# A list scheduler that ranks by due time instead of program order, with durations as traced

## The chip, the cores and the metric

One core of a Trainium2 chip runs the whole kernel. The core has TensorE (PE, matmuls; PEld is its weight load), VectorE (DVE), ScalarE (ACT), GpSimd (POOL) and SyncE (SP), whose queue issues all of this kernel's DMAs. The metric is the time of one execution in device microseconds, as the median of the runs.

## The reference

One layer of an encoder over 1024 tokens of width 1024, in float32:

```python
for l in range(DEPTH):   # DEPTH = 1
    mod = (silu(c) @ ada_w[l] + ada_b[l]).reshape(B, 3, 3, D_MODEL)
    h = modulate(x, norm_g[l, 0], mod[:, 0, 0], mod[:, 0, 1])        # RMS norm, scale, shift
    x = x + 0.5 * mod[:, 0, 2] * swiglu(h, ffn1_w1[l], ffn1_w3[l], ffn1_w2[l])
    h = modulate(x, norm_g[l, 1], mod[:, 1, 0], mod[:, 1, 1])
    y = hybrid_mixer(h, ...)
    x = x + mod[:, 1, 2] * y
    h = modulate(x, norm_g[l, 2], mod[:, 2, 0], mod[:, 2, 1])
    x = x + 0.5 * mod[:, 2, 2] * swiglu(h, ffn2_w1[l], ffn2_w3[l], ffn2_w2[l])
```

The feed-forward width is 2816. The mixer projects h to queries, keys and values of two kinds of attention with 8 heads of 64 each: one with a forget gate and a causal mask ("fox"), one in which each query attends to the 256 keys with the highest index score (the top-k part, "dsa"). Their outputs go through a projection each, are weighted by sigmoid gates of h, added and projected again.

## The kernel before, in words

Every float32 product is made of three fp32r matmuls: an operand is split into a high part (`wh`, `h`, `yh`, `pth`; ACT copies it to fp32r) and a low part (`wl`, `yl`, `ptl`; DVE or POOL subtracts), and `mm3` issues high x high, high x low, low x high. A feed-forward product is made by Strassen's scheme with 7 instead of 8 block products, so DVE also adds and subtracts blocks of weights (`wr`, `a`, `s`), of operands (`t1` to `t4`) and of results (`z`, `u`).

The layer function describes the work in program order in five parts, each ended by a `flush`: the modulation and the first feed-forward, with the first projections of the mixer; index scores and the first two groups of fox heads; the other projections, half of the gates and the top-k search (`topk`, 32 rounds of counting on DVE and 33 on ACT); attention (`pt` transposes of probabilities, `pth` and `ptl` their split, `py` the value products), with the other half of the gates between (`gt`, whose matmuls write `py` tiles too) and the masks; the branches' projections (`wbr`, `d_y`), the mixer's output and the second feed-forward.

The program calls nothing directly. `Plan.take` (line 182) records each instruction as a `Task` with its predecessors, and gives it a rank: its place in program order plus `behind`, an amount by which some side work (modulation 150, gates and top-k 100, masks 600) is set back. `Plan.flush` (line 264) then places the tasks of its part one by one. For each engine it goes through up to 60 waiting tasks, ordered by rank, and picks the one that can start earliest; a later one in that order is taken only if it can start over 0.05 us earlier. Of the engines' picks the earliest is placed. The start is the latest of: the inputs' end, the engine's, the buffers' and, for DVE and POOL, the other's use of the shared port. A task that takes a new tile has to wait while its rank is over `window` (200, from the second part on 600) above the lowest rank not yet placed. `Plan.length` (line 246) gives the duration of an instruction, and 0.12 us are added before another engine may use the result. A DMA takes 1.3 us and its bytes at 345 KB per us, one after another, and 0.7 us. The order found is the order in which each engine gets its instructions; the chip waits on semaphores, not on the planned times. Nothing else depends on the plan but which buffer of a pool a tile gets.

All instructions are issued from one line, 358, so groups of the profile are told apart by their tiles.

Of the kernel before, what the change touches and what calls it, by code (L numbers as in the profile page):

```python
# [18 lines left out]
PSUM = bass.MemoryType.PSUM  # L19
# [36 lines left out]
class View:  # L56
# [53 lines left out]
    def real(self):  # L110
        t = self.tile.real()
        for name, a, kw in self.ops:
            t = t[a[0]] if name == "__getitem__" else getattr(t, name)(*a, **kw)
        return t
# [45 lines left out]
    return v.real() if isinstance(v, View) else v  # L160


class Plan:


# [16 lines left out]
    def take(self, engine, op, a, kw):  # L182
        if not self.on:
            return getattr(getattr(self.tc.nc, engine), op)(*map(real, a), **{n: real(v) for n, v in kw.items()})
        t = Task(len(self.tasks), engine, op, a, kw)
        t.rank = t.i + self.behind
        self.tasks.append(t)
        writes = [v for v in (a[0], kw.get("accum_out")) if isinstance(v, View)]
        reads = [v for v in list(a[1:]) + [w for n, w in kw.items() if n != "accum_out"] if isinstance(v, View)]
        before = set()  # L190
        for views, write in ((reads, False), (writes, True)):
            for v in views:
                r = v.region()
                for r2, j, w2 in v.tile.log:
                    if (write or w2) and j != t.i and all(p < q2 and p2 < q for (p, q), (p2, q2) in zip(r, r2)):
                        before.add(j)
        for views, write in ((reads, False), (writes, True)):
            for v in views:
                if write and not v.ops:
                    v.tile.log = []  # L200
                v.tile.log.append((v.region(), t.i, write))
        t.ready = max([getattr(v.tile, "written", 0.0) for v in reads] + [0.0])
        tiles = {id(v.tile): v.tile for v in reads + writes + self.wanted}
        self.wanted = []
        for x in tiles.values():
            if x.t is None and x.first is None:
                t.new.append(x)
                x.first = t.i
            elif x.t is None:
                before.add(x.first)  # L210
            x.uses += 1
        t.tiles = list(tiles.values())
        t.written = [v.tile for v in writes]
        for j in before:
            self.tasks[j].after.append(t)
        t.left = len(before)
        out = writes[0] if writes else a[0]
        shape = list(out.shape)
        t.n = int(np.prod(shape[1:]))
        if op == "tensor_reduce":  # L220
            t.n = int(np.prod(a[1].shape[1:]))
        t.bytes = 4 * int(np.prod(shape))
        t.port = engine in ("vector", "gpsimd") and "accum_out" not in kw and not any(
            v.tile.pool.space == PSUM for v in reads + writes)
        if engine == "tensor":
            m = a[2] if op == "matmul" else a[1]
            t.exact = m.tile.dt in (F32R, BF16) or any(o[0] == "bitcast" and F32R in o[1] for o in m.ops)
# [16 lines left out]
        return self.done.setdefault(x.key, [(0.0, i) for i in range(x.kw.get("bufs", 1))])  # L244

    def length(self, t, e):
        if e == "tensor":
            if t.exact:
                return max(0.08, t.n / 2250.0)
            if t.op == "transpose":  # L250
                return t.n / 860.0
            return max(0.24, t.n / 500.0)
        more = "accum_out" in t.kw
        if e == "scalar":
            return 0.1 + t.n / 1200.0 + (0.3 if more else 0.12 if any(isinstance(t.kw.get(x), View) for x in ("bias", "scale")) else 0.0)
        if e == "vector":
            if t.op == "tensor_tensor_scan":
                return 0.1 + t.n / 450.0
            return max(0.2, 0.08 + t.n / 960.0 + (0.18 if more else 0.06 if t.op == "scalar_tensor_tensor" else 0.0))
        if e == "gpsimd":  # L260
            return 0.1 + t.n / (900.0 if t.op == "tensor_scalar" else 440.0)
        return 0.35

    def flush(self, keep=()):

# [3 lines left out]
        tasks, free = self.tasks, self.free  # L269
        start = max(free.values())  # L270
        waiting = {e: [] for e in self.ENGINES}

        def release(t):
            insort(waiting[t.engine], t, key=lambda u: u.rank)

        for t in tasks:
            if not t.left:
# [7 lines left out]
        def slot(t):  # L285

            when, need = 0.0, {}
            for x in t.new:
                if x.kw.get("tag"):
                    need.setdefault(x.key, []).append(x)  # L290
            if need and t.rank > low + self.window:
                return None
            for s, xs in need.items():
                if xs[0].kw["bufs"] == 1 and news[s][0] != t.i:
                    return None
                got = sorted(self.slots(xs[0]))
                if len(got) < len(xs) + (0 if news[s][0] == t.i else min(self.spare, xs[0].kw["bufs"] // 4)):
                    return None
                when = max(when, got[len(xs) - 1][0])
            return when  # L300

        todo = sorted(tasks, key=lambda t: t.rank)
        while len(order) < len(tasks):
            best = None
            while todo[0].placed:
                todo.pop(0)
            low = todo[0].rank
            for e in self.ENGINES:
                w = waiting[e][:60]
                pick, ahead = None, 0.0  # L310
                for t in w:
                    room = slot(t) if t.new else 0.0
                    if room is None:
                        continue
                    s = max(t.ready, room, free[e])
                    if t.port:
                        s = max(s, self.port["gpsimd" if e == "vector" else "vector"])
                    if pick is None or s < pick[0] - 0.05:
                        pick = (s, t, e)
                if pick and (best is None or pick[0] < best[0]):  # L320
                    best = pick
            assert best, "no task can be placed: " + str([(t.engine, t.op, [x.kw for x in t.new]) for w in waiting.values() for t in w][:8])
            s, t, e = best
            d = self.length(t, e)
            end = s + d + 0.12
            if t.port:
                self.port[e] = s + d
            free[e] = s + d
            if e == "sync":
                self.wire = max(self.wire, s + 1.3) + t.bytes / 345e3  # L330
                end = self.wire + 0.7
                free[e] = max(free[e], self.wire - 5.0)
            t.placed = True
            order.append((s, len(order), t, e, d))
            waiting[e].remove(t)
            for x in t.new:
                if x.kw.get("tag"):
                    news[x.key].remove(t.i)
                    x.slot = min(self.slots(x))
                    self.slots(x).remove(x.slot)  # L340
                    x.slot = x.slot[1]
            for x in t.written:
                x.written = max(getattr(x, "written", 0.0), end)
            for x in t.tiles:
                x.uses -= 1
                x.end = max(getattr(x, "end", 0.0), end)
                if not x.uses and x.slot is not None:
                    self.slots(x).append((x.end, x.slot))
                    self.kept.pop(id(x), None)
            for u in t.after:  # L350
                u.left -= 1
                u.ready = max(u.ready, s + d if u.engine == e and e != "sync" else end)
                if not u.left:
                    release(u)
        self.trace = sorted(order, key=lambda o: o[:2])
# [151 lines left out]
def t512(k, dt=F32, name="t", home="c"):  # L507

    p, tag, n = k.homes[home]
    return p.tile([128, H], dt, tag=tag, name=name, bufs=n)  # L510
# [1057 lines left out]
class Down:  # L1568
# [34 lines left out]
    def sum(self, n, q):  # L1603
        a, nc = {m: t[q] for m, t in self.a.items()}, self.k.nc
        if n == "s3":
            self.any.tensor_sub(a["a11"], a["a11"], a["a21"])
        elif n == "s2":
            t = self.a["s2"][q] = t512(self.k, name="s2")
            self.any.tensor_sub(t, a["a22"], a["a11"])
        elif n == "s1":  # L1610
            self.any.tensor_add(a["a21"], a["a21"], a["a22"])
        elif n == "s4":
            self.any.tensor_sub(a["a12"], a["a12"], a["s2"])
# [665 lines left out]
```

## Time and profile before

| | |
|---|---|
| runs | 2271.02, 2266.53, 2259.95 us |
| median of the runs | 2266.53 us |
| span of the profiled execution | 2259.4 us |
| mean granted clock of TensorE | 0.989 |
| TensorE busy, matmuls | 2178.7 us, 10508 |
| weight loads busy | 1799.5 us |
| DVE busy, instructions | 1802.3 us, 3391 |
| ACT busy, instructions | 1101.8 us, 1996 |
| POOL busy, instructions | 268.6 us, 255 |
| HBM read, written | 237.53 MB, 76.28 MB |

The profile is of one more execution; its span runs from the first to the last instruction, and no time of its own is listed beside it. It is 7.1 us below the median of the runs and 0.6 us below the lowest. A row of a stretch gives its bounds in us from the span's start, its length, and for each engine the busy us and the instructions that started in it. Busy time of TensorE includes modelled ends of pipelined matmuls: its mean for one matmul of 512 columns is 396 ns, while 2618 of them start in 600 us.

### The profile page before, as it was taken

The numbers are of one execution on the slowest core, as the hardware profiler recorded it, in microseconds if no ns is written. First come the engines' busy times: TensorE is split into PE (matmuls) and PEld (weight loads), VectorE is DVE, ScalarE is ACT, GpSimd is POOL, SyncE is SP. The second block draws the span as 40 slices with busy tenths as digits, with TensorE's granted clock in tenths as the row PEclk, the third lists the DMA queues.
The fourth block names the chain that finished last, engine by engine and source line by source line (L and its number), as shares of the span: only waits on it lengthen the run. The fifth ranks groups of instructions, "written<-read, shape, count | busy, mean of one in ns | idle before, by whom it ended". The sixth has DMA issues, their size and how long they took to land.

```text
span 2259.4 us, 31187 instructions
## 1 busy us (share of the span) xinstructions
PE 2178.7 (96%) x10508; PEld 1799.5 (80%) x10508; DVE 1802.3 (80%) x3391; ACT 1101.8 (49%) x1996; POOL 268.6 (12%) x255
## 2 busy tenths in 40 slices
PE   7999999999999999998999999899999999999999
PEld 5777888787887989996778887687888888888887
DVE  7998987889775488888788877668898877769765
ACT  4432232344464476787687787423443333324443
POOL 0000000000010223323555433000000000000000
PEclk9999999999999999999999999999999999999999
DMA  9234554497421313334332210767223442258520
GB/s 336 81 114 161 168 173 131 146 367 238 126 74 61 121 61 122 113 122 136 107 110 89 76 35 20 278 239 256 87 80 131 135 133 96 93 179 319 168 75 38
DMA packets 187421, 315.89 MB, mean 140 GB/s; under 512 B 27366, under 2 KB 51942, under 8 KB 187260
## 3 DMA queue, kind: packets, MB, share of 16 engines
q1 hardware_dynamic: 187260, 313.89, 41.1%
q8 instruction: 83, 1.36, 0.2%
q14 instruction: 78, 0.64, 0.1%
HBM read 237.53 MB, written 76.28 MB: 139 GB/s over the span
## 4 chain that ended last, share of the span: by engine, by line
PE 45%; DVE 3%; ACT 2%; DMA 2%; issue 1%; SPq 0%; ACTq 0%; DVEq 0%; POOL 0%
PE b L358 34%; PE py L358 6%; PE pt L358 3%; PE p L358 2%; DVE macc L358 1%; DMA wr<-in_w_g 1%; DMA mraw<-in_ada_w 0%; ACT pth L358 0%; ACT pr L358 0%; DVE ptl L358 0%; ACT kst L358 0%; DVE qs L358 0%; DMA wr<-in_wbr 0%; ACT yt L358 0%; DVE kst L358 0%
## 5 line engine op out<-in xcount | busy, mean ns | idle before, releaser
L358 PE MATMUL b<-h,wh 128*128 128x512 f32 x2720 | 855.8, 396 | 10.0 <-ACT wh L358 5.0
L358 PEld LDWEIGHTS b<-h,wh 128*128 128x128 f32 x2720 | 511.9, 189 | 136.1 <-ACT wh L358 9.1
L358 PE MATMUL b<-h,wl 128*128 128x512 f32 x1360 | 533.7, 395 | 2.4 <-DVE wl L358 2.4
L358 ACT ACTIVATE wh<-wr 128x512 fp32r<-128x512 f32 (+2 forms) x368 | 245.5, 676 | 469.3 <-PE b L358 343.8
L358 PEld LDWEIGHTS b<-h,wl 128*128 128x128 f32 x1360 | 256.2, 188 | 64.2 <-DVE wl L358 4.2
L358 DVE TENSOR_TENSOR z<-b,z 128x512 f32<-128x512 f32 x308 | 207.3, 684 | 73.0 <-PE b L358 71.9
L358 PE MATMUL b<-wl,wh 128*128 128x512 f32 x616 | 241.8, 393 | 5.5 <-DVE wl L358 5.5
L358 PE MATMUL b<-wh 128*128 128x512 f32 x616 | 239.4, 391 | 2.5 <-ACT wh L358 1.7
L358 PE MATMUL b<-wh,wl 128*128 128x512 f32 x616 | 241.2, 392 | 0.0
L358 DVE TENSOR_TENSOR wl<-wr,wh 128x512 fp32r<-128x512 f32 x312 | 206.7, 683 | 32.9 <-ACT wh L358 32.8
L358 PE MATMUL pj<-wh,h 128*128 128x384 f32 (+1 forms) x768 | 179.5, 319 | 0.1
L358 ACT ACTIVATE wh<-a 128x512 fp32r<-128x512 f32 x132 | 83.3, 631 | 194.0 <-PE b L358 168.3
L358 POOL TENSOR_TENSOR wl<-wr,wh 128x1024 fp32r<-128x1024 f32 (+2 forms) x56 | 120.1, 2150 | 283.8 <-ACT wh L358 276.9
L358 DVE TENSOR_TENSOR wl<-a,wh 128x512 fp32r<-128x512 f32 x132 | 91.4, 693 | 76.8 <-ACT wh L358 76.8
L358 PEld LDWEIGHTS b<-wl,wh 128*128 128x128 f32 x616 | 116.6, 189 | 31.9 <-DVE wl L358 7.6
L358 PEld LDWEIGHTS b<-wh 128*128 128x128 f32 x616 | 116.1, 188 | 27.8 <-ACT wh L358 2.3
L358 PEld LDWEIGHTS b<-wh,wl 128*128 128x128 f32 x616 | 116.4, 189 | 24.6 <-DVE wl L358 0.4
L358 PEld LDWEIGHTS pj<-wh,h 128*128 128x128 f32 x768 | 132.4, 188 | 1.1 <-ACT wh L358 0.2
L358 DVE TENSOR_TENSOR z<-z 128x512 f32<-128x512 f32 x176 | 119.4, 690 | 10.7 <-DVE z L358 0.5
L358 PE MATMUL pj<-wl,h 128*128 128x384 f32 (+1 forms) x384 | 122.6, 319 | 0.5 <-POOL wl L358 0.5
L358 POOL TENSOR_SCALAR pr<-pr,mn 128x128 f32<-128x128 f32 (+7 forms) x128 | 101.2, 804 | 153.7 <-DVE mn L358 136.8
L358 DVE TENSOR_TENSOR wl<-g,wh 128x512 fp32r<-128x512 f32 x154 | 106.7, 695 | 0.0
(283 smaller groups left out, 3677.3 us busy)
## 6 DMA issues: line engine op xcount, KB each, us to landing
d_g<-z SPq DMA_DIRECT2D x154, 256.0 KB
g<-d_g SPq DMA_DIRECT2D x154, 256.0 KB
mraw<-in_ada_w SPq DMA_DIRECT2D x144, 256.0 KB
wr<-in_w13a SPq DMA_DIRECT2D x112, 256.0 KB
wr<-in_w13b SPq DMA_DIRECT2D x88, 256.0 KB
wr<-in_w_g SPq DMA_DIRECT2D x32, 512.0 KB
a<-in_w2a SPq DMA_DIRECT2D x44, 256.0 KB
a<-in_w2b SPq DMA_DIRECT2D x44, 256.0 KB
```

What stands on the lines that cost most here:

```text
L358: getattr(getattr(self.tc.nc, e), t.op)(*map(real, t.a), **{n: real(v) for n, v in t.kw.items()})
```

## The change

`flush` orders waiting tasks by a due time, `due`, in place of the rank. `deadlines` works it out before each part is placed. It goes through the tasks by rank and lays the matmuls and transposes end to end: one is due when the sum of the durations ahead of it says. Any other task is due 20 us (`SLACK`) after the matmuls ahead of it in rank. Then it goes backward: a task is due no later than the due time of each task that uses its result, less its own duration, less the time that a result takes to another engine, and for a DMA less 2.0 us and its bytes. A task that uses a tile whose buffer a later tile will take over (`soft`) is due ahead of the task that takes it. The rule of the 0.05 us, the 60 tasks, the window and the ranks themselves stay.

`length` returns two numbers, duration and time to another engine: for 512 columns a matmul takes 0.230 (before 0.228), a transpose of 128 columns 0.109 (0.149), a DVE operation on two tensors 0.603 (0.613), an ACT copy 0.537 (0.527). A result takes 0.23 us from TensorE, 0.16 from ACT, 0.145 from DVE, 0.105 from POOL (0.12 before, whatever the engine). ACT with a running sum takes 0.1 us more in place of 0.3. 0.03 us is added for each engine over one that a task waits for. A use on the same engine after a running sum waits 0.1 us. The shared port of DVE and POOL is now taken by a POOL task that reads more than 8 columns from SBUF, and by a DVE task that reads two such inputs from SBUF, or one in `tensor_scalar`, `tensor_copy` and `reciprocal`; before it was by every task of the two engines that has no PSUM tile and no running sum.

```diff
@@ -158,6 +158,9 @@
 
 def real(v):
     return v.real() if isinstance(v, View) else v
+SLACK = 20.0
 
 
 class Plan:
@@ -213,6 +216,7 @@
         t.written = [v.tile for v in writes]
         for j in before:
             self.tasks[j].after.append(t)
+        t.waits = len({self.tasks[j].engine for j in before} - {engine})
         t.left = len(before)
         out = writes[0] if writes else a[0]
         shape = list(out.shape)
@@ -220,8 +224,17 @@
         if op == "tensor_reduce":
             t.n = int(np.prod(a[1].shape[1:]))
         t.bytes = 4 * int(np.prod(shape))
-        t.port = engine in ("vector", "gpsimd") and "accum_out" not in kw and not any(
-            v.tile.pool.space == PSUM for v in reads + writes)
+        wide = [v for v in reads if int(np.prod(v.shape[1:])) > 8]
+        sb = [v for v in wide if v.tile.pool.space != PSUM]
+        if engine == "gpsimd":
+            t.port = bool(sb)
+        elif engine == "vector":
+            if op in ("tensor_scalar", "tensor_copy", "reciprocal"):
+                t.port = len(sb) == 1 and "accum_out" not in kw and writes[0].tile.pool.space != PSUM
+            else:
+                t.port = len(sb) >= 2
+        else:
+            t.port = False
         if engine == "tensor":
             m = a[2] if op == "matmul" else a[1]
             t.exact = m.tile.dt in (F32R, BF16) or any(o[0] == "bitcast" and F32R in o[1] for o in m.ops)
@@ -244,22 +257,84 @@
         return self.done.setdefault(x.key, [(0.0, i) for i in range(x.kw.get("bufs", 1))])
 
     def length(self, t, e):
+        n = t.n
+        if e == "sync":
+            return 0.06, 0.0
         if e == "tensor":
             if t.exact:
-                return max(0.08, t.n / 2250.0)
-            if t.op == "transpose":
-                return t.n / 860.0
-            return max(0.24, t.n / 500.0)
+                d = max(0.04, 0.009 + n / 2317.0)
+            elif t.op == "transpose":
+                d = n / 1174.0
+            else:
+                d = max(0.224, 0.009 + n / 595.0)
+            return d, 0.23
         more = "accum_out" in t.kw
         if e == "scalar":
-            return 0.1 + t.n / 1200.0 + (0.3 if more else 0.12 if any(isinstance(t.kw.get(x), View) for x in ("bias", "scale")) else 0.0)
-        if e == "vector":
-            if t.op == "tensor_tensor_scan":
-                return 0.1 + t.n / 450.0
-            return max(0.2, 0.08 + t.n / 960.0 + (0.18 if more else 0.06 if t.op == "scalar_tensor_tensor" else 0.0))
+            ap = sum(isinstance(t.kw.get(x), View) for x in ("bias", "scale"))
+            return 0.11 + n / 1200.0 + (0.1 if more else 0.0) + (0.06 if ap else 0.0), 0.16
         if e == "gpsimd":
-            return 0.1 + t.n / (900.0 if t.op == "tensor_scalar" else 440.0)
-        return 0.35
+            if t.op in ("tensor_scalar", "memset"):
+                return 0.08 + n / 960.0, 0.105
+            return 0.06 + n / 440.0, 0.105
+        if t.op == "tensor_tensor_scan":
+            d = 0.15 + n / 480.0
+        elif t.op == "tensor_tensor_reduce":
+            d = 0.17 + n / 960.0
+        elif t.op == "scalar_tensor_tensor" or more:
+            d = 0.13 + n / 960.0
+        elif t.op == "tensor_scalar" and t.port:
+            d = 0.075 + n / 1920.0
+        else:
+            d = 0.07 + n / 960.0
+        return max(0.2, d), 0.145
+    def deadlines(self):
+        tasks = self.tasks
+        at = 0.0
+        ordered = sorted(tasks, key=lambda t: t.rank)
+        for t in ordered:
+            t.len, t.lat = self.length(t, t.engine)
+            if t.waits > 1 and t.engine not in ("tensor", "sync"):
+                t.len += 0.03 * (t.waits - 1)
+            t.due = at + SLACK
+            if t.engine == "tensor":
+                t.due = at
+                at += t.len
+        users, frees, soft, born, ends, count = {}, {}, {}, {}, {}, {}
+        for t in ordered:
+            for x in t.tiles:
+                users.setdefault(id(x), []).append(t)
+        for t in ordered:
+            for x in t.new:
+                born[id(x)] = x
+        for n, t in enumerate(ordered):
+            t.pos = n
+        for i, ts in users.items():
+            ends.setdefault(ts[-1].pos, []).append(i)
+        for t in ordered:
+            for x in t.new:
+                if not x.kw.get("tag"):
+                    continue
+                q = frees.setdefault(x.key, [])
+                n = count.get(x.key, 0)
+                if n < x.kw["bufs"]:
+                    count[x.key] = n + 1
+                elif q:
+                    for u in users[q.pop(0)]:
+                        if u.pos < t.pos:
+                            soft.setdefault(u.pos, []).append(t)
+            for i in ends.get(t.pos, ()):
+                if i in born and id(born[i]) not in self.kept and born[i].kw.get("tag"):
+                    frees.setdefault(born[i].key, []).append(i)
+        for t in reversed(ordered):
+            d = t.due
+            for u in t.after:
+                d = min(d, u.due - t.len - (t.lat if u.engine != t.engine else 0.0) - (2.0 + t.bytes / 345e3 if t.engine == "sync" else 0.0))
+            for u in soft.get(t.pos, ()):
+                d = min(d, u.due - t.len - t.lat)
+            t.due = d
 
     def flush(self, keep=()):
 
@@ -269,9 +344,10 @@
         tasks, free = self.tasks, self.free
         start = max(free.values())
         waiting = {e: [] for e in self.ENGINES}
+        self.deadlines()
 
         def release(t):
-            insort(waiting[t.engine], t, key=lambda u: u.rank)
+            insort(waiting[t.engine], t, key=lambda u: u.due)
 
         for t in tasks:
             if not t.left:
@@ -321,8 +397,8 @@
                     best = pick
             assert best, "no task can be placed: " + str([(t.engine, t.op, [x.kw for x in t.new]) for w in waiting.values() for t in w][:8])
             s, t, e = best
-            d = self.length(t, e)
-            end = s + d + 0.12
+            d = t.len
+            end = s + d + t.lat
             if t.port:
                 self.port[e] = s + d
             free[e] = s + d
@@ -349,7 +425,7 @@
                     self.kept.pop(id(x), None)
             for u in t.after:
                 u.left -= 1
-                u.ready = max(u.ready, s + d if u.engine == e and e != "sync" else end)
+                u.ready = max(u.ready, s + d + (0.1 if "accum_out" in t.kw else 0.0) if u.engine == e and e != "sync" else end)
                 if not u.left:
                     release(u)
         self.trace = sorted(order, key=lambda o: o[:2])
```

## The prediction, made before the changed kernel ran

> **What bounds the kernel now.** I read the page's first part, then a table of stretches, then the groups by shape in the attention stretch, then the chain, the waits and the timeline at the places where TensorE stops.
>
> ```profile
> span 2259.4 us, 31187 instructions
> PE 2178.7 (96%) x10508; PEld 1799.5 (80%) x10508; DVE 1802.3 (80%) x3391; ACT 1101.8 (49%) x1996; POOL 268.6 (12%) x255
> ```
>
> TensorE is the bound, with 4% idle by this line. But a busy TensorE is not a dense one: ends of matmuls are modelled, and they overlap. So I count matmuls per stretch. Columns: length, then busy us (x instructions) of PE, PEld, DVE, ACT and POOL, granted clock, DMA share, GB/s.
>
> ```profile
> 0.00:28.00 28.00, 14.87 (x50) 6.34 (x51) 15.96 (x38) 10.43 (x17) 0.69 (x6) 1.00 0.94 338
> 28.00:100.00 72.00, 71.99 (x326) 59.61 (x325) 69.69 (x123) 36.25 (x63) 0.00 (x0) 0.98 0.56 192
> 100.00:250.00 150.00, 141.15 (x582) 110.23 (x581) 138.23 (x242) 48.73 (x82) 0.50 (x2) 0.97 0.40 134
> 550.00:850.00 300.00, 283.70 (x1405) 249.06 (x1404) 209.35 (x345) 159.15 (x271) 38.54 (x31) 0.99 0.29 95
> 1045.00:1075.00 30.00, 20.62 (x86) 16.33 (x85) 19.73 (x64) 20.42 (x37) 13.68 (x13) 0.81 0.42 139
> 1075.00:1370.00 295.00, 285.35 (x1799) 232.74 (x1798) 240.11 (x540) 221.65 (x472) 144.09 (x157) 1.00 0.26 80
> 1370.00:1421.00 51.00, 41.91 (x271) 34.77 (x268) 36.73 (x88) 35.48 (x80) 14.82 (x20) 0.97 0.09 23
> 1421.00:1428.00 7.00, 0.02 (x1) 0.02 (x1) 2.64 (x4) 3.14 (x6) 0.00 (x0) 0.56 0.91 292
> 1428.00:1560.00 132.00, 129.60 (x553) 104.31 (x553) 103.69 (x164) 46.75 (x77) 0.00 (x0) 0.98 0.82 284
> 1560.00:2160.00 600.00, 600.00 (x2618) 488.23 (x2617) 474.95 (x776) 225.13 (x371) 0.00 (x0) 1.00 0.42 143
> ```
>
> The stretch 1560:2160, the second feed-forward, is dense: 600 / 2618 = 0.229 us for a matmul of 512 columns. There no order of work can gain anything. At that pace 100:250 has room for 654 matmuls and holds 582: 72 x 0.229 = 16.5 us are lost, with VectorE busy 138 of 150 us, so VectorE is what TensorE waits for there. 1428:1560 has room for 576 and holds 553: 5 us lost. 550:850, where forms are mixed, has at least 300 - 283.7 = 16 us idle. 1045:1075 has 9 us idle, and the rest at 0.81 of the clock.
>
> In attention the count needs shapes. The groups of 1100 to 1400, kept apart by shape (count | busy us, mean ns | idle before):
>
> ```profile
> L358 PE MATMUL pt<-ident,pr 128*128 128x128 f32 x512 | 80.9, 276 | 4.9 <-DVE kst L358 2.1 <-DVE qs L358 1.5 <-DVE ptl L358 1.2
> L358 PE MATMUL py<-h,wh 128*128 128x512 f32 x202 | 71.0, 407 | 0.0
> L358 PE MATMUL py<-pth,vst 128*128 128x256 f32 x171 | 53.9, 322 | 2.1 <-ACT pth L358 1.8
> L358 PE MATMUL py<-ptl,vst 128*64 128x256 f32 x171 | 46.1, 292 | 1.4 <-DVE ptl L358 1.2
> L358 PE MATMUL py<-h,wl 128*128 128x512 f32 x101 | 41.6, 412 | 0.0
> L358 PE MATMUL py<-pzh,vst 128*128 128x256 f32 x112 | 34.1, 304 | 0.8 <-ACT pzh L358 0.5
> L358 PE MATMUL p<-kst,qs 128*128 128x512 f32 x84 | 28.1, 418 | 0.0
> L358 PE MATMUL py<-pzl,vst 128*64 128x256 f32 x112 | 23.0, 287 | 0.4 <-DVE pzl L358 0.4
> L358 PE MATMUL p<-kst,qs 128*128 128x384 f32 x84 | 21.7, 354 | 0.0
> L358 PE MATMUL p<-kst,qs 128*128 128x448 f32 x56 | 17.3, 396 | 0.0
> L358 PE MATMUL p<-kst,qs 128*128 128x320 f32 x56 | 13.2, 334 | 0.1
> L358 PE MATMUL pt<-ident,nat 128*128 128x128 f32 x68 | 11.6, 274 | 0.2
> ```
>
> A row of the chain of work that ended last prices a transpose (eight in 0.87 us, 0.109 each):
>
> ```profile
> 1249.90 0.87 PE pt L358 x8
> ```
>
> By columns at 0.229 per 512: 202 + 101 + 84 = 387 of 512, 89 us; 171 + 171 + 112 + 112 = 566 of 256, 65 us; 84 of 384, 56 of 448 and 56 of 320 together 33.5 us; 512 + 68 = 580 transposes, 63 us; some 10 for the smaller groups left out, an estimate from their counts. Sum 260 of 300 us: 40 us, 13%, are gaps of a few tenths that the busy share hides. Scaled to 1075:1421 that is 46 us.
>
> **The change, part by part.** No instruction is added or removed: 10508 matmuls, 3391 VectorE and 1996 ACT instructions should stay; only their order on each engine and the order of the DMAs on SP's queue change. So the sum consists of stalls taken away or added.
>
> First, prices. A transpose was planned at 128/860 = 0.149 us and is now 128/1174 = 0.109, as the row shows; over the 512 of the groups above the old plan reserved 20 us of TensorE that the chip did not need, where it put no gate matmul. A 512-column matmul goes from 0.2276 to 0.230, right by the dense row. For a hop from ACT to VectorE:
>
> ```profile
> 1424.86 0.63 ACT L358 ACTIVATE wh<-wr 128x512 fp32r<-128x512 f32 x1 [1.13 <-DMA wr<-in_wbr]
> 1425.58 0.69 DVE L358 TENSOR_TENSOR wl<-wr,wh 128x512 fp32r<-128x512 f32 x1 [1.06 <-ACT wh L358]
> ```
>
> Start to start 0.72 us; the old plan had 0.10 + 0.427 + 0.12 = 0.647, the new one has 0.697. A VectorE split goes from 0.733 to 0.748 with its hop. For a chain transposes, pth, ptl, values that is 2.10 before and 2.11 after, since the shorter transposes pay for the longer hops; so prices alone free no latency, they only tell the planner where TensorE has room.
>
> Second, order. Work with equal start was picked by program rank; now by due time. The gain falls where an engine has several tasks ready and TensorE starves.
>
> (a) 0:28. DMA is busy at 0.94, 338 GB/s; the same bytes must land first. Gain 0, bounds -2 to +2.
>
> (b) 100:250. VectorE holds operands, splits, partial sums of the modulation and z sums; those that no matmul needs soon get the 20 us of slack. VectorE is 92% busy, so about 8% of 150 us, 12 us, is its own slack; but 28:100 is at 97% already and its backlog comes along. I take 6 of 16.5; bounds 0 and 14.
>
> (c) 550:850. The statistics of the norm, the last sums and the first small parts; VectorE has 70%, so it is latency and order. I take 5 of 16; bounds 0 and 12.
>
> (d) 1045:1075. These rows of the timeline and of the top-k threshold's tile (first and last start):
>
> ```profile
> 1046.12 0.39 PE L358 MATMUL pj<-h,wl 128*128 128x512 f32 x1
> 1044.97 7.22 SPq L358 DMA_DIRECT2D d_gate<-gt  x2
> 1052.39 1.94 PE L358 MATMUL pt<-ident,nat 128*128 128x128 f32 x8 [5.89 <-issue]
> L358 DVE TENSOR_TENSOR thr<-tkku,tkm x1: 465/465/465, 1062.9 to 1062.9; 128x3 uint32<-128x3 uint32 x1
> ```
>
> TensorE stops at 1046.5 for 5.9 us while SP's queue holds two gate stores; transposes stand ahead of gate matmuls that could run. Stores get a late due time, loads an early one, so some of it should go: 3 us. Against it: top-k ends 16 us behind the last matmul of its plan, its rounds get 20 us of slack, and attention's VectorE work queues behind them. Bounds -15 (it slides by the slack, less the gate matmuls that cover 5) and +9.
>
> (e) Attention, 1075:1421, 46 us in gaps. These waits and the gate group's last start (first and last start in the row):
>
> ```profile
> PEld py L358 <- ACT pth L358: 15.4, 42, 1.9
> PEld py L358 <- DVE ptl L358: 10.3, 28, 0.5
> L358 PE MATMUL py<-h,wl x128: 387/395/628, 1055.0 to 1370.5; 128*128 128x512 f32 x128
> ```
>
> TensorE waits for a piece of probability to be split, in 70 waits. The cover is 384 gate matmuls, 88 us, and it is used up at 1370; the next 51 us have 9 us idle even by the busy count. With attention's tasks due early by their chain and gate matmuls due late, the cover is spread to the end; with transposes priced right, about half of the 20 us reserved is filled. But gate tiles share the py banks with attention's sums, which no order changes. I take 14 of 46: 10 for the half of 20, 4 of the 9. Bounds -5 (a gate holding a bank when values want it) and +30.
>
> (f) 1421:1428. The branch weights' loads, four, stand ahead of the first y tiles:
>
> ```profile
> 1421.01 5.65 DMA wr<-in_wbr
> PE b L358 <- ACT yh L358: 10.0, 1, 10.0
> ```
>
> The first products need one of the four weights and one y. By due time three loads fall behind. 256 KB each at 292 GB/s, 0.9 us: 2.7, I take 3; bounds 0 and 4.
>
> (g) 1428:1560: 1 of 5; bounds 0 and 4. Stretches that are dense: 0; they are covered as long as splits and loads run ahead, and cost what the second rival says if not.
>
> Sum: 0 + 6 + 5 + 3 + 14 + 3 + 1 = 32 us off the span of 2259.4, 2227. The runs shown are 2259.95 to 2271.02 with median 2266.5, 7 us above that span; the same off the median gives 2234.5. All upper bounds together: 2 + 14 + 12 + 9 + 30 + 4 + 4 = 75, 2191. All lower ones: +22, 2288.
>
> A rule weighed. By PEld's share, 1075:1370 has 232.74 / 295 = 78.9% against 488.23 / 600 = 81.4% where it is dense, which would leave 9 us to win there, not 40. The Trainium skill, "Perfetto Trace Analysis", section Identifying the Most-Contended Engine, says to judge TensorE's headroom by the busy share of weight loads, not by that of matmuls. By that rule term (e) would be about 3. The count speaks against it: a 256-column matmul takes 0.115 us of pace and still has one whole weight load, so loads fill time there that matmuls do not. I take the count, and keep the other as a rival.
>
> **The rivals.** No change: picking is greedy by earliest start, and rank or due time decides only between tasks that could start within 0.05 us of each other. For it: ACT is 49% busy, so its queue seldom holds two. Against: VectorE's 92% in 100:250. Time: 2266, within 8.
>
> Slower: the look-ahead closes. A task that takes a new tile waits until the lowest unplaced rank is within 200. Rank order places low ranks first; due order leaves a task without a matmul behind it for 20 us and more. At 2618 + 776 + 371 instructions in 600 us, 6.3 per us and some DMAs, 200 ranks are about 30 us. Where VectorE is above 90% such a task starves, loads stop, and TensorE waits for a load and both splits, some 4 us (2.7 of bytes and issue, 0.63, 0.69). Its place is the first feed-forward to 550, and the second one. It eats the gain at 8 such waits; at 15 the time is 2234.5 + 60 = 2294. For it: 28:100 and 100:250 are at 97% and 92%. Against: 1560:2160 has VectorE at 79%.
>
> Attention is nearly full, as PEld's share has it: 3 instead of 14, so 21 us off, 2245.
>
> **How the numbers follow.** 0.5%, 11 us, is what a measurement of this kernel can tell from no change. Chances: forecast 0.57, time 2234; attention nearly full 0.11; no change 0.16; look-ahead closes 0.16. The first two are faster (0.68), the third the same, the fourth slower. The forecast's own range is 2200 to 2255. The whole range reaches from 2198 (a few in a hundred lie below, since the bounds will not all be met together) to 2276, which takes in no change and the mild cases of closing; about 0.15 lie outside.
>
> **What would show it.** Right: more than 600 matmuls in the 150 us after 100; the last gate matmul within 25 us of the last attention matmul; the first branch matmul under 7 us after the last value product; the dense stretch still at 0.229. Wrong: the last threshold more than 20 us behind the last gate matmul of its plan; waits of TensorE for wh or wl of 3 us and more in the feed-forwards, which would be the look-ahead closing; or the same count in attention, 13% of gaps, which would say that banks and not order hold it.

## The result, and the profile after

The changed kernel takes 2230.6 us, against 2265.0 for the kernel before on the same chip: a ratio of 0.985, 95% interval 0.983 to 0.987. Forecast were 2234 and "faster". The sum was right by luck: up to the last index score 31 us were won where the prediction took 11, in top-k and attention 4 were lost where it took 17 to be won, and the two errors cancel.

The page of the changed kernel, its first lines:

```profile
span 2226.2 us, 31118 instructions
PE 2160.8 (97%) x10508; PEld 1800.5 (81%) x10508; DVE 1802.2 (81%) x3391; ACT 1097.5 (49%) x1996; POOL 271.1 (12%) x255
```

From PE to POOL not one instruction is added or lost; the 33 us by which the span is shorter are stalls. The same stretches, moved to where the same work now lies (length, busy us and count of PE, PEld, DVE, ACT, POOL, then granted clock, DMA share, GB/s):

```profile
28.00:100.00 72.00, 72.00 (x328) 59.91 (x327) 69.60 (x122) 37.23 (x65) 0.00 (x0) 0.98 0.52 183
100.00:250.00 150.00, 149.25 (x635) 118.25 (x634) 141.84 (x254) 48.88 (x83) 0.50 (x2) 1.00 0.44 142
530.00:850.00 320.00, 312.95 (x1587) 278.94 (x1586) 240.71 (x428) 172.95 (x297) 47.42 (x34) 1.00 0.32 102
850.00:1043.00 193.00, 176.65 (x973) 158.01 (x971) 164.50 (x464) 143.91 (x270) 49.05 (x25) 0.96 0.33 106
1043.00:1075.00 32.00, 26.19 (x156) 22.09 (x156) 25.03 (x62) 24.16 (x51) 21.21 (x23) 0.89 0.58 177
1075.00:1370.00 295.00, 286.48 (x1875) 244.30 (x1874) 247.77 (x561) 232.20 (x496) 147.17 (x160) 1.00 0.25 77
1370.00:1391.00 21.00, 18.26 (x119) 15.44 (x116) 14.21 (x30) 13.53 (x28) 5.04 (x6) 0.92 0.11 28
1391.00:1398.00 7.00, 0.03 (x1) 0.00 (x0) 1.11 (x2) 1.10 (x3) 0.00 (x0) 0.67 0.60 155
1528.00:2128.00 600.00, 600.00 (x2618) 488.27 (x2618) 473.74 (x783) 225.51 (x373) 0.00 (x0) 1.00 0.43 143
```

100:250 holds 635 matmuls in place of 582, with VectorE hardly busier (142 us in place of 138): it does more of what TensorE waits for and less of the rest. From 28 us on to the same 931 matmuls it had done 213.7 us of work before (28:256) and has done 204.6 now (28:243). The second feed-forward has 2618 in 600 us again. And 850:1043, the stretch of top-k and first gates, has 16 us of idle TensorE where the kernel before had none:

```profile
850.00:1045.00 195.00, 195.00 (x1124) 178.79 (x1123) 170.90 (x500) 148.62 (x274) 56.25 (x28) 1.00 0.35 118
```

Behind it, in 1043:1075, TensorE idles 5.8 us in place of 9.4, but its longest stall there stays: 6.2 us, before 5.9.

Windows at fixed times mix causes, so I cut every run at the same pieces of work. The bounds are starts of matmuls: the last of the first feed-forward, the last index score, the last `pj` (projections and first gates), the last `py` (attention), the first branch product, the last of all. "top-k late" says by how much the last write of the thresholds comes after the last `pj`. A row is one traced execution: three kernels below that plan the first feed-forward as the changed one does (e4, e8, e9) take 680.7 to 683.5 us there, so 3 us in one part can be chance.

| us | first feed-forward | index | top-k part | attention | to branches | rest | top-k late |
|---|---|---|---|---|---|---|---|
| before | 706.3 | 137.7 | 202.1 | 371.6 | 10.2 | 827.1 | 16.8 |
| changed | 681.0 | 132.0 | 229.2 | 348.5 | 7.7 | 823.4 | 2.7 |
| difference | -25.3 | -5.7 | +27.1 | -23.1 | -2.5 | -3.7 | |

So 37 us are won outside top-k and attention. These two together take 573.7 before and 577.7 after: nothing is won there at all, though the boundary between them moved by 25 us.

### The profile page after: what moved, and what is told of

Its sections match the earlier page's. It is cut to its first block, busy times and chain, and to the rows that moved or that the text cites. A ratio compares the mean times of both kernels' runs of the same rounds, so it can differ in the third digit from the quotient of the medians.

```text
span 2226.2 us, 31118 instructions
## 1 busy us (share of the span) xinstructions
PE 2160.8 (97%) x10508; PEld 1800.5 (81%) x10508; DVE 1802.2 (81%) x3391; ACT 1097.5 (49%) x1996; POOL 271.1 (12%) x255
## 4 chain that ended last, share of the span: by engine, by line
PE 76%; DVE 15%; DMA 3%; ACT 3%; issue 2%; SPq 1%; POOL 0%; DVEq 0%; ACTq 0%
PE b L434 60%; PE py L434 6%; PE pt L434 3%; PE p L434 3%; PE pj L434 3%; DVE tkj L434 3%; DVE z L434 2%; DMA wr<-in_w13a 1%; DVE wl L434 1%; DVE qkv L434 1%; DVE s L434 1%; DVE wr L434 1%; DVE h L434 1%; DVE tkkey L434 1%; SPq L434 1%
## 5 line engine op out<-in xcount | busy, mean ns | idle before, releaser
L434 PE MATMUL pj<-wh,h 128*128 128x384 f32 (+1 forms) x768 | 185.9, 325 | 13.9 <-ACT gt L434 13.4
L434 POOL TENSOR_SCALAR pr<-pr,mn 128x1024 f32<-128x1024 f32 (+7 forms) x128 | 100.5, 800 | 132.0 <-DVE mn L434 76.0
L434 ACT ACTIVATE pr<-pr,mn 128x896 f32<-128x896 f32 (+7 forms) x128 | 98.8, 773 | 17.4 <-DVE mn L434 16.6
```

Source lines behind the costliest of these rows:

```text
L434: getattr(getattr(self.tc.nc, e), t.op)(*map(real, t.a), **{n: real(v) for n, v in t.kw.items()})
```

## The experiments

Each kernel ran in turn with the kernel before on the same chip (2264.6 to 2266.3 us). The edits are against the changed kernel.

| kernel | us | ratio (95%) | first feed-forward | index | top-k part | attention | top-k late |
|---|---|---|---|---|---|---|---|
| e1_narrow | 2271.8 | 1.004 (1.003 to 1.005) | 682.1 | 134.5 | 223.8 | 395.6 | 10.2 |
| e2_rank | 2260.6 | 0.998 (0.997 to 0.999) | 703.3 | 140.1 | 224.6 | 350.0 | 3.7 |
| e3_old_prices | 2232.8 | 0.987 (0.985 to 0.988) | 684.5 | 133.7 | 204.9 | 373.3 | 22.0 |
| e4_part4_rank | 2235.0 | 0.987 (0.986 to 0.989) | 683.1 | 131.6 | 234.8 | 348.7 | 4.5 |
| e5_accum | 2225.4 | 0.983 (0.981 to 0.986) | 681.5 | 131.8 | 224.2 | 352.3 | 7.5 |
| e6_old_port | 2238.6 | 0.989 (0.986 to 0.991) | 682.7 | 131.6 | 214.3 | 375.1 | 11.5 |
| e7_transpose | 2234.2 | 0.987 (0.984 to 0.989) | 683.1 | 131.2 | 229.2 | 354.8 | 2.7 |
| e8_mix | 2224.7 | 0.983 (0.980 to 0.986) | 680.7 | 132.0 | 207.0 | 366.7 | 22.0 |
| e9_half_rounds | 2220.1 | 0.980 (0.979 to 0.982) | 683.5 | 131.5 | 225.1 | 343.3 | -11.8 |
| e10_dve_due | 2271.4 | 1.004 (1.002 to 1.005) | 684.0 | 150.1 | 230.8 | 366.0 | 4.4 |
| e11_pieces | 2240.4 | 0.989 (0.988 to 0.991) | 683.9 | 129.6 | 243.4 | 346.6 | 1.9 |
| e12_topk_first | 2227.5 | 0.983 (0.981 to 0.985) | 682.4 | 131.8 | 224.3 | 352.6 | 5.5 |

**Order or prices.** One kernel keeps the new prices and goes back to ranks, one keeps due order and takes back every price, hop and port rule:

```diff
-            insort(waiting[t.engine], t, key=lambda u: u.due)
+            insort(waiting[t.engine], t, key=lambda u: u.rank)
```

> New prices, ports and hops, but every part ordered by program rank. If order makes the gain: little moves against before in the first feed-forward (14 us) and in the norm after it (11 us), and the time is 2245 to 2262 us, attention giving what there is. If prices make it: 2230 to 2240 us.

```diff
     def length(self, t, e):
+        return self.old(t, e), 0.12        # length of the kernel before; its port rule too
```

> Due order with the old prices, port rule and 0.12 us hops. If order makes the gain: the 25 us up to the first projections are kept; attention keeps about half of its 23 us; the part of top-k does not lose 27 us by theory N, since narrow operations count for the port again, and does by theory O. So 2215 us by N and order, 2240 us by O and order, 2255 us or more if prices make the gain.

Ranks with new prices win 4 us, due order with old prices 32 (2232.8), both 34 (2230.6). The order is the gain. By the parts it lies in the first feed-forward (703.3 with ranks, 684.5 with old prices, 681.0 with both), the index part and the rest. In the two middle parts the prices move the boundary: the top-k part takes 202 and 205 us with old prices and 225 and 229 with new ones, attention 372 and 373 against 350 and 349. By expectation the top-k part would lose by order or by narrow operations; up to its last `pj` it does not lose by order. But order alone keeps nothing of attention's 23 us, and misses both 2215 and 2240. And counted from the last index score to the last `pj` or the last threshold, whichever is later, order alone loses too: 218.9 us before, 226.9 with order alone, 228.3 with prices alone, 231.9 with both.

**Whose order.** Due time on VectorE's queue alone:

```diff
-            insort(waiting[t.engine], t, key=lambda u: u.due)
+            insort(waiting[t.engine], t, key=lambda u: u.due if u.engine == "vector" else u.rank)
```

> The changed kernel with VectorE's queue alone ordered by due time, the other four by rank. By the prediction's steps for the first feed-forward and the norm, VectorE's order is what gains there: 681 to 687 us up to the end of the first feed-forward (703 with rank on all queues, 681 with due on all). Rival: the order of loads on SP's queue or of TensorE's own matmuls gains; then 695 or more.

684.0: 19 of the 22 us that order wins in the first feed-forward come from VectorE's queue, the rest is within chance. After it this kernel loses everything again (150 in the index part, 366 in attention): why, no run tells; that its queues follow two different orders is a guess. TensorE's waits from 28 us on in the first feed-forward, first before (to 550), then changed (to 530); they name ACT, which made the operand last, and it is the edit, not these rows, that points at VectorE:

```profile
PE b L358 <- ACT wh L358: 5.0, 3, 3.8
PE b L358 <- ACT h L358: 4.9, 3, 2.7
```

```profile
PE b L434 <- ACT wh L434: 0.3, 1, 0.3
PE b L434 <- DVE wl L434: 0.2, 1, 0.2
```

**What the top-k part lost.** The changed kernel around the longest wait of this part, on PE, ACT, DVE and POOL in turn:

```profile
936.09 0.58 PE L434 MATMUL pj<-wh,h 128*128 128x256 f32 x1 [6.87 <-ACT gt L434]
```

```profile
934.31 1.15 ACT L434 ACTIVATE tks<-tkh,tkca 128x1024 bf16<-128x1024 uint16 x1 [4.25 <-DVE tkca L434]
935.37 0.19 ACT L434 ACTIVATION_READ_ACCUMULATOR tks<-tkh,tkca 128x1 f32 x1
935.46 0.57 ACT L434 ACTIVATE gt<-pj 128x512 f32<-128x512 f32 x1
```

```profile
930.34 2.15 DVE L434 TENSOR_TENSOR tkv<-tksgn,tklim 128x3 f32<-128x3 f32 x1
932.53 0.16 DVE L434 SCALAR_TENSOR_TENSOR tkkey<-tkv,tkkey 128x3 f32<-128x3 f32 x1
```

```profile
930.14 2.34 POOL L434 TENSOR_TENSOR wl<-wr,wh 128x1024 fp32r<-128x1024 f32 x1 [2.10 <-ACT wh L434]
```

Read from below: a GpSimd split starts at 930.14; a VectorE operation on 3 columns, otherwise 0.16 us, takes 2.15, to the split's end. That is 2.0 us of delay; four more VectorE operations, 1.6 us, come before the bound `tkca`. The sign pass at the head of ACT's queue waits 4.25 us for it, and the gate's tanh stands behind the sign pass. Its PSUM bank stays taken, and TensorE waits 6.87 us for a bank. The sums over the part: ACT's sign passes waiting for a bound, first before (844:1046), then changed (813:1043), and TensorE's waits in the changed kernel, of which the kernel before had none on `pj`:

```profile
ACT tks L358 <- DVE tkca L358: 17.4, 5, 11.8
```

```profile
ACT tks L434 <- DVE tkca L434: 42.8, 15, 7.4
PE pj L434 <- ACT gt L434: 13.4, 4, 6.9
PE pj L434 <- ACT qkv L434: 2.5, 1, 2.5
```

The new port rule leaves out operations of 8 columns or fewer, so the plan does not know of the block. Counting them again, and ordering this part alone by rank (it is the fourth of the plan's six flushes, for the norm with the first projections has one of its own):

```diff
-        wide = [v for v in reads if int(np.prod(v.shape[1:])) > 8]
+        wide = reads
```

> The changed kernel, but a VectorE operation with narrow operands (8 columns or fewer) takes the shared port in the plan as well. Theory N: the 27 us lost between the last index score and the last gate of the first half come from unplanned blocks of narrow top-k operations by GpSimd splits (one of 0.15 us takes 2.15 us), which hold a sign pass on ACT and the gate's tanh queued behind it; then the four waits for that tanh (13.4 us) go and the time falls to about 2208 us. Theory O: due order as such puts top-k ahead and crowds ACT; then the time stays at 2231 within 6 us.

```diff
         self.deadlines()
+        self.part = getattr(self, "part", 0) + 1
+        if self.part == 4:
+            for t in tasks:
+                t.due = t.rank
```

> The changed kernel with the part of top-k and first gates alone ordered by rank again, all prices new. Theory O: the 27 us of that part come back and the rest of the gain stays, about 2205 us. Theory N: the narrow operations are still planned as unblocked, so at most half comes back: 2217 to 2231 us.

Theory O falls: ranks make the part longer, 234.8. Theory N gets 5 us of the 27, TensorE's waits on `pj` for `gt` and `qkv` go only from 15.9 to 12.3 us, and attention loses 47. Why attention loses is not shown. Counting every narrow operation also keeps the softmax's reciprocals, two columns wide, away from GpSimd in the plan, while the chip did not hold them up (last section); and by this edit a `tensor_scalar` with a one-column operand has two inputs and no longer takes the port, so the edit changes more than the narrow operations. Then two prices apart:

```diff
-            ... + (0.1 if more else 0.0) + (0.06 if ap else 0.0), 0.16
+            ... + (0.29 if more else 0.06 if ap else 0.0), 0.16
-        elif t.op == "scalar_tensor_tensor" or more:
+        elif more:
+            d = 0.26 + n / 960.0
+        elif t.op == "scalar_tensor_tensor":
```

> The changed kernel with the old prices for operations with a running sum alone: ACT 0.40 us and VectorE 0.26 us above the columns (the change has 0.27 and 0.13). Theory A: the 25 us that the new prices lose in the top-k part come from the second instruction that reads the accumulator, which the new prices leave out, some 0.13 us for each of 99 sign passes and 96 counts; then that part takes 205 to 212 us in place of 229 and the whole 2207 to 2215. Rival P: they come from the port rule; then the part stays at 225 to 230 us and the time at 2231.

```diff
-        wide = [v for v in reads if ...]          # the new rule, 10 lines
+        t.port = engine in ("vector", "gpsimd") and "accum_out" not in kw and not any(
+            v.tile.pool.space == PSUM for v in reads + writes)
```

> The changed kernel with the old rule for the shared port alone. Theory P for attention: its 23 us come from narrow operations and those with one SBUF input no longer being planned around GpSimd; then attention goes from 349 back to 368 to 375 us, and the whole to about 2252. Rival T: they come from the transposes' price; attention stays at 349. For the top-k part: by theory A it stays at 225 to 230 us, by rival P it falls to 205.

A sign pass is underpriced, as this timeline of the changed kernel's ACT shows (start, length):

```profile
938.98 1.13 ACT L434 ACTIVATE tks<-tkl,tkca 128x1024 bf16<-128x1024 uint16 x1
940.01 0.19 ACT L434 ACTIVATION_READ_ACCUMULATOR tks<-tkl,tkca 128x1 f32 x1
940.23 1.04 ACT L434 ACTIVATE tks<-tkl,tkca 128x896 bf16<-128x896 uint16 x1
```

1.25 us from one to the next; the old price is 1.253, the new one 1.123, since the second instruction that reads the sum was left out. The old price brings 5 of the 27 us (224.2), so theory A falls short; the old port rule brings 15 (214.3), short of P's 205 but the larger share, and attention then loses 27 us, as P expected there. To the later of the last `pj` and the last threshold the gains are smaller still: 231.7 and 225.7 us against 231.9. All old prices in this part alone:

```diff
     def length(self, t, e):
+        if self.part == 4:
+            return self.old(t, e), 0.12           # and the old port rule, in this part alone
```

> Due order everywhere, the old prices, hops and port rule in the part of top-k and first gates alone, the new ones elsewhere. If the parts stand by themselves: 204 us for that part, 349 for attention, 681 up to the norm; about 2205 us. If what that part leaves behind (its last gates, the last threshold) changes attention: 2215 us or more.

The waits for a bound shrink and those on `pj` all but go (813 to 1042, ACT and PE), while TensorE stands for 10.5 us right behind the last `pj`:

```profile
ACT tks L458 <- DVE tkca L458: 11.3, 6, 4.1
```

```profile
PE pt L458 <- issue: 10.5, 1, 10.5
PE pj L458 <- ACT qkv L458: 0.7, 1, 0.7
```

The part takes 207.0. That the new prices and rule make the loss up to the last `pj` is shown. How they make it is in part argued: that an order planned without the blocks and reads puts sign passes ahead of evacuations on ACT. The blocks themselves do not tell the kernels apart: up to the last threshold 12 two-input operations on at most 8 columns took over 0.4 us in the kernel before (16 us over the usual 0.16), 13 in the changed one (18) and 16 here (24), though the old rule counts them. What differs is how long the sign passes wait for a bound (11.3 us here, 17.4 before, 42.8 in the changed kernel) and what stands behind them. And the 22 us go into the next part: attention 366.7, the whole 2224.7.

**Why the two parts share one sum.** Top-k ends 22 us after the last `pj` there; attention's work for VectorE is placed behind it. Counted from whichever ends later, attention takes 354.8 us before, 351.3 with due order and old prices, 346.2 with ranks and new prices, 345.8 with both, 344.6 in the mixed kernel. So its own gain is 9 us; 14 of the 23 are the top-k part's end moved. Ranks with new prices have all but 0.4 of the 9, so order adds nothing to them there. Of the 9, the transposes' price:

```diff
-                d = n / 1174.0
+                d = n / 860.0
```

> The changed kernel with a transpose priced at 0.149 us again. By the prediction's step, half of the 20 us reserved for transposes in attention was filled: attention then loses about 10 us, 2241. By theory T it loses all 23, 2254. By theory P for attention nothing moves beyond 4 us, 2231.

gives 6 (352.1 from the later end, 354.8 by the table), less than the prediction's 10 and far from the 23 of theory T; the whole, 2234.2, cannot be told from 2230.6. Attention in the kernel with the old port rule takes 363.7 from the later end, 18 more: beside the other new prices the new rule is worth that much there, while with all prices old attention takes 351.3.

From the last index score to that later end the times are 218.9 before and 231.9 changed. What sets it?

```diff
-        for bit in range(31, -1, -1):
+        for bit in range(31, 15, -1):
```

> The changed kernel with 16 of the 32 counting rounds on VectorE left out (the thresholds of three query blocks are then coarse): some 47 us less VectorE work in the top-k part. From the last index score to the last value product every kernel but two took 574 to 584 us, however the top-k part and attention shared it. Theory V: VectorE's work for top-k is what that sum waits for; it falls by 25 us or more, and the whole to 2205 or less. Rival L: the chain of 33 sign rounds on ACT, or TensorE itself, sets it; it falls by less than 10 us.

```diff
-    k.lo_eng.tensor_sub(lo[:, :n], raw[:, :n], hi[:, :n].bitcast(F32))
+    for j in range(0, n, 256):
+        s = slice(j, j + 256)
+        k.lo_eng.tensor_sub(lo[:, s], raw[:, s], hi[:, s].bitcast(F32))
```

> The changed kernel with GpSimd's split of mixer weights cut into pieces of 256 columns (0.6 us each in place of one of 2.4). Where a narrow VectorE operation with two inputs falls into such a split it takes 1.2 to 2.4 us in place of 0.16, 28 us in all in the top-k part. Theory V with these blocks: they shrink to under 10 us, the sum of top-k part and attention falls by 10 to 20 us, the whole to 2212 to 2221. Rival L: the blocks are slack; 2231 within 5, or slower by GpSimd's extra starts.

Theory V falls: 47 us less VectorE work shorten the two parts by 9 us (568.4), and the top-k part by 4. Shorter GpSimd pieces block more two-input operations on at most 64 columns (46 in place of 20 over 0.4 us, up to the last threshold) for 22 us over the usual 0.16 in place of 30, and lose 10 us. What remained was the chain on ACT, 33 rounds of three passes: from the first to the last pass 195 us before, 211 changed, 192 with half of the counting. Last, on top of the accumulator prices, top-k not set back:

```diff
-            beside(behind(nc, topk(k, tp), 100), 66, ...)
+            beside(behind(nc, topk(k, tp), 0), 66, ...)
```

> The changed kernel with the old prices for running sums (2225 us) and top-k no longer set back by 100 ranks. From the first to the last sign pass ACT takes 208 us there, 195 before the change and 192 with half of the counting rounds. Theory L: this chain of 33 rounds, each waiting on VectorE for its next bound, is what the part waits for; with top-k due some 15 us earlier, VectorE gives the bound sooner, the chain takes 195 us or less, and the whole 2210 to 2218. Rival: gate and projection evacuations on ACT are then later still, TensorE waits for banks, and the time is 2225 or more.

The chain stays at 209 us (208 without this edit) and the time at 2227.5; the rival's 2225 or more holds, though its reason does not, as TensorE's waits for `qkv` (10.7 and 10.2 us) and `gt` (2.1 and 1.9) are the same. So this run did not shorten the chain and does not test it. Half of the counting did (192 us), and the two parts became only 9 us shorter, with 12.4 us of waits for `gt` left; and with shorter pieces the chain is as long as in the changed kernel (210), yet the later end comes 13 us later. That the chain alone sets the top-k part is therefore not borne out; what sets it stays open.

The two fastest kernels that compute the whole layer, 2224.7 and 2225.4, are 5 us below the changed one, and their intervals overlap with its own.

## Why the prediction was right, and where it was not

(a) The start: first product at 27.6 us before, 27.3 now, as said: 0.

(b) 100:250: more than 600 matmuls were to show it; 635 do. The 600th `h,wh` product of this part starts 13.2 us earlier, twice the 6 taken, inside the bounds 0 and 14. Most of it came as the prediction says, by work put off: to the same 931 matmuls VectorE has done 9 us less. The rest is 4 us less idle time, so its own slack of 12 us, named as the limit, was not what limited it.

(c) 550:850: from the 500th down product (15.7 us ahead) to the last index score (31.0 ahead) 15 us are won, where 5 was taken and 12 was the upper bound. The bound came from halving the 16 us of idle TensorE; stalls hidden in the busy share, which the count showed for attention, were not looked for here.

(d) and (e), the step that failed. The prediction took 3 + 14 there and 0 for 850:1045, because that stretch was dense. The three together gave 4 us more, not 17 less. In attention the half of its mechanism that rests on the transposes' price is borne out in size (6 us, 10 taken); the half that rests on order, gate matmuls spread as cover, is not, since ranks do as well. By its own count of matmuls 1075:1375 now has 27 us in gaps, 9% in place of 13%. What it lacked is that dense TensorE in 850:1045 rested on an order, lost with the new prices and back in the mixed kernel, in which TensorE did not wait for gate and projection evacuations behind sign passes on ACT; "0; they are covered" named splits and loads as the cover and not the evacuations. It also listed the prices of running sums and the port rule in the change's description and costed neither. Its bound for top-k's slack, 15 us later, had the right sign but the wrong place: from the last index score the last threshold comes 13 us later, yet 14 us nearer to the last `pj`, because the projections end 27 us later.

That the gate matmuls would be spread to attention's end is wrong: the last gate matmul starts at 1331.0 and the last value product 60 us later, 47 before.

```profile
L434 PE MATMUL py<-h,wh x256: 387/396/776, 1050.4 to 1331.0; 128*128 128x512 f32 x128
L434 PE MATMUL py<-ptl,vst x192: 276/281/562, 1066.5 to 1390.3; 128*64 128x256 f32 x192
```

(f) The loads by due time: one branch weight now goes ahead of seven y tiles, and the first product follows the last value product after 7.7 us in place of 10.2: 2.5, with 3 taken. "Under 7 us" was missed by 0.7; the weight still lands 5.83 us after ACT is ready:

```profile
1392.54 0.46 SPq L434 DMA_DIRECT2D wr<-in_wbr  x1
1397.80 0.63 ACT L434 ACTIVATE wh<-wr 128x512 fp32r<-128x512 f32 x1 [5.83 <-DMA wr<-in_wbr]
```

(g) 3.7 with what follows, 1 taken.

The rival of the closing look-ahead did not come: no wait for a split of 3 us is left in the feed-forwards, and the dense stretch has its 0.229. "No change" by greedy picking is refuted by the 19 us of VectorE's queue. The runs do not decide on the weight-load share as a measure of room: the 9 us that it left in attention are what attention won from its later end, but the share of 1075:1370 is now 244.30 / 295 = 82.8%, above the 81.4% of the dense stretch, so it is no measure of a full engine across these sizes.

## What to carry to other kernels

Due times carried back from the bound engine paid here on the engine that is nearly as busy as it and serves several masters: VectorE in the first feed-forward. A price list that is nearer to the trace in most places can plan a worse order: here a waiting instruction came to the head of an in-order queue, and what stood behind it held the bound engine. A missing accumulator read and a missing lock have a part in it; they do not account for all of it. When one part gains what its neighbour loses, measure both from the later of the two ends before calling it a gain.

## What the runs showed of the hardware

In the changed kernel 29 VectorE operations on at most 64 columns with two inputs start during a GpSimd split; 23 of them take over 0.35 us, up to 2.34, and the median of the 29 is 1.25; the 290 others have a median of 0.16 and none is over 0.23. So an operation on three columns can be held to the end of a split of a thousand, as the rows at 930 show. None of the 64 reciprocals on two columns, one input, is longer than 0.17, though 25 of them start during GpSimd's work. The Trainium skill, "SBUF — State Buffer", section Who interferes with whom, says that a VectorE operation with two SBUF inputs and a GpSimd operation that reads SBUF exclude each other for a whole instruction, and that one with a single input does not take part outside the two-port modes. The traces agree, for operations on three columns too. In some runs narrow `tensor_scalar` operations, one input, were held up too (over 0.35 us: 4 of 5 in the kernel that counts narrow operations, 5 of 7 in the kernel before).
